# Hybrid decoder layer: weight pairs split inside the softmax, mixer products later, the last head's transposes behind six output products of two token tiles

## Chip, cores and metric

The kernel runs on one core of a Trainium2 chip. The metric is the device time of one execution in microseconds (us). The engines are named as the profile names them: PE (TensorE), PEld (its weight load), DVE (VectorE), ACT (ScalarE), POOL (GpSimd), SP (SyncE, here a queue of DMA issues).

## What is computed

One layer over 512 tokens of 1024 channels, in float32. The part that the change touches is the first sub-layer:

```python
h = rms_norm(x, g_mix_pre)
u, q, k, v = split(h @ w_in)                  # 512 channels each
y_pool = pool_mixer(u, w_pool, pool_scale)    # 4 groups: trailing mean over 2/4/8/16 tokens minus the
                                              # token, then a 128x128 product and a scale per channel
y_attn = moba_attention(q, k, v, rel_bias)    # 8 heads of 64; at 512 tokens: causal attention with bias
x = x + rms_norm(concat(y_pool, y_attn) @ w_out, g_mix_post)
x = x + rms_norm(conv_ffn(rms_norm(x, g_ffn_pre)), g_ffn_post)
x = x + (p @ w_ple) * sigmoid(x @ w_ple_gate)
```

## The kernel before

**Three matmuls for a product.** Every float32 operand is split into a rounded part (hi) and the rest (lo). `mm3` (L222) issues three matmuls for a product: hi and lo crosswise, then hi with hi. For activations `split` (L228) makes the pair: ACT copies the rounded part, DVE subtracts it from the source.

**Weights.** `_Weights` (L68) holds the order of all weight chunks (1 MB each). A chunk is loaded by SP into one of two raw buffers and split in two halves; each half gives a pair (`wh`, `wl`), of which six fit. `ahead(n)` (L122) splits until n pairs lie ahead of the one last taken: a copy on ACT (L147), a subtraction on DVE (L148), and after a chunk's second half the load of the chunk two further on. `take()` hands out the next pair. Pairs 8 to 15 are u0, u1, q2, k2, q3, k3, u2, u3 of the input projection; 16 to 19 are the left half of `w_out` (512 output columns), two blocks of 128 rows in each; 20 to 23 the right half.

**Attention.** There is no scheduler: each engine runs its instructions in the order in which the program issues them. For head h: `scores(h)` (L442) is 8 matmuls on PE, then for the four token tiles on DVE bias, mask and minimum (L454), on ACT the exponential with its sum (L456), on DVE one reciprocal (L457) and four multiplications (L460) that finish the probabilities `L`. `transposes(h)` (L469) turns the ten blocks of `L` on PE into PSUM, and `split` brings them to `PT`. `values(h)` (L486) is 8 matmuls with `V`, and ACT and DVE bring the result into rows of `yT`. Heads come in pairs that share a block of 128 channels: `query` and `key` (L413, L422) project such a pair into `QK`, and `spread` (L429) copies it by DMA to `ST`, from which the scores read.

The loop over h = 0 to 6 (L556) issues the `fills` of h (a projection of 24 matmuls, with which PE passes the time of a softmax; after it `W.ahead(3)`), `transposes(h)`, `scores(h+1)`, and `values(h)`. `pool_in(g)` (L508) projects mixer group g and has POOL make the trailing means; `pool_mid(g)` splits the result, `pool_out(g)` (L529) is the mixer's product (3 matmuls), whose result ACT and DVE bring to block g of `yT`.

**Output product.** `out_part(t, n, ks, ...)` (L571) multiplies token tile t with blocks ks of `w_out` for column half n, three matmuls a block. Blocks 0 to 3 of `yT` are the mixer's, 4 to 7 are heads 0-1, 2-3, 4-5, 6-7. While head 7 is unfinished the blocks `part` = (4, 5, 0, 1, 6) of the four token tiles are multiplied, and after it (2, 3, 7). The order at the end of the attention is:

```python
wo = [W.take() for _ in range(4)]          # L576, after W.ahead(4) behind values(6)
out_part(0, 0, part, True, False)
transposes(H - 1)
out_part(1, 0, part, True, False)
pool_out(2, "pt")
values(H - 1)
pool_mid(3)
out_part(2, 0, part, True, False)
pool_out(3, "pt")
out_part(3, 0, part, True, False)
```

Of the kernel before, what the change touches and what calls it, by code (L numbers as in the profile page):

```python
# [17 lines left out]
F32 = mybir.dt.float32  # L18
F32R = mybir.dt.float32r
# [5 lines left out]
P = 128  # L25
# [42 lines left out]
class _Weights:  # L68
# [31 lines left out]
    def load(self, between=None):  # L100
# [10 lines left out]
        else:  # L111
# [4 lines left out]
            for i in range(n):  # L116
                part = slice(i * step, (i + 1) * step)
                self.nc.sync.dma_start(self.raw[c][:, part, :], src[:, part, :])
                if between is not None:
                    between(i)  # L120

    def ahead(self, n):  # L122

        while self.split < min(self.used + n, 2 * len(self.chunks)):
            c, s = divmod(self.split, 2)
            while self.loaded <= c:
                self.load()
            srcs, axis = self.chunks[c]
            if axis is None:
                view = srcs[s][0]  # L130
            elif axis in (0, 3):
                view = self.raw[c][:, s, :srcs[s].shape[1], :]
            else:
                raw = self.raw[c]
                half = raw.shape[axis] // 2
                part = slice(s * half, (s + 1) * half)
                view = raw[:, part, :] if axis == 1 else raw[:, :, part]
            pair = []
            for kind in "hl":
                t = self.pool.tile([P, 1024], F32R, tag="w" + kind, name=f"w{kind}{self.split}", bufs=self.PAIRS)  # L140
                size = view.shape[1] * view.shape[2]
                pair.append(t[:, :size].rearrange("p (a b) -> p a b", a=view.shape[1]))
            if axis is None:
                for t, src in zip(pair, srcs[s]):
                    self.nc.sync.dma_start(t.bitcast(F32), src)
            else:
                self.nc.scalar.copy(pair[0], view)  # L147
                self.nc.vector.tensor_sub(pair[1], view, pair[0].bitcast(F32))  # L148
            self.pairs[self.split] = pair
            self.split += 1  # L150
            if s == 1:
                self.raw.pop(c, None)
                while self.loaded < min(c + 1 + self.RAW, len(self.chunks)):
                    self.load()

    def take(self):
        self.ahead(1)
# [5 lines left out]
def hybrid_layer(ctx, tc, x, p, rel_bias, g_mix_pre, g_mix_post, g_ffn_pre, g_ffn_post, w_in, w_pool,  # L163
# [23 lines left out]
    for c in (768, 896):  # L187
        W.two(w_in, c, c + 512)
    W.cols(w_in, 256)
    for n in range(2):  # L190
        for k0 in (0, 4):
            W.rows(w_out, k0, 4, 512 * n, 512)
    for fb in range(NF // 2):
        W.cols(w_up, 256 * fb)
        W.cols(w_up, FF + 256 * fb)
# [203 lines left out]
    def project(name, tag="mm", n=3):  # L399
        w = W.take()  # L400
        ps = bank(name, tag)
        for k in range(KD):
            mm3(ps, [q[:, k, :] for q in w], h_moving(k), k == 0, k == KD - 1)
        W.ahead(n)
        return ps
# [4 lines left out]
    QK = ap2.tile([P, 4, S], F32R, name="qk")  # L410
    ST = [[ap2.tile([P, S], F32R, name=f"q_{e}"), ap2.tile([P, 2, S], F32R, name=f"k_{e}")] for e in range(2)]

    def query(hp, spread_now=False):  # L413
        ps = project(f"q{hp}", n=0 if spread_now else 3)
        act.mul(QK[:, 0, :], ps, -(DH ** -0.5))
        dve.scalar_tensor_tensor(QK[:, 3, :], ps, -(DH ** -0.5), QK[:, 0, :].bitcast(F32), op0=ALU.mult,
                                 op1=ALU.subtract)
        if spread_now:
            spread("q")
            W.ahead(3)  # L420

    def key(hp, spread_now=False):  # L422
        ps = project(f"k{hp}", n=0 if spread_now else 3)
        split([QK[:, 1, :], QK[:, 2, :]], ps)
        if spread_now:
            spread("k")
            W.ahead(3)

    def spread(what):  # L429


        for e in range(2):
            src = slice(e * DH, (e + 1) * DH)
            for w in what:
                for a in range(2):
                    dst = ST[e][w == "k"][a * DH:(a + 1) * DH]
                    cs = slice(1, 3) if w == "k" else 0 if a == e else 3
                    sp.dma_start(dst.bitcast(F32), QK[src, cs, :].bitcast(F32))
# [3 lines left out]
    def scores(h):  # L442
        q, k = ST[h % 2]
        bk = [bank(f"s{h}_{b}", "s") for b in range(3)]
        for i, (b, c, _) in place.items():
            n = (i + 1) * P
            for a in (1, 0):
                pe.matmul(bk[b][:, c:c + n], q[:, i * P:n], k[:, a, :n], start=a == 1, stop=a == 0)
        L[h] = ap2.tile([P, 1280], F32, tag="L", name=f"L{h}", bufs=1)
        m = small.tile([P, 12], F32, tag="m", name=f"m{h}", bufs=2)  # L450
        for i, (b, c, o) in place.items():
            n = (i + 1) * P
            l = L[h][:, o:o + n]
            dve.tensor_tensor_reduce(out=l, in0=bk[b][:, c:c + n], in1=T[:, h, S - n:], scale=1.0, scalar=MASKED,  # L454
                                     op0=ALU.add, op1=ALU.min, accum_out=m[:, i:i + 1])
            act.activation(l, l, AF.Exp, bias=m[:, i:i + 1], scale=-1.0, accum_out=m[:, 4 + i:5 + i])  # L456
        dve.reciprocal(m[:, 8:], m[:, 4:8])  # L457
        for i, (b, c, o) in place.items():
            l = L[h][:, o:o + (i + 1) * P]
            dve.tensor_scalar_mul(l, l, m[:, 8 + i:9 + i])  # L460
# [47 lines left out]
    def pool_in(g):  # L508

        w = 2 << g  # L510
        ps = project(f"u{g}", n=4 if g == 2 else 3)
        act.copy(ub[0][:, 16:], ps)  # L512
        src = ub[0]
        for lvl in range(g + 1):
            nxt = ub[1 + lvl % 2]
            pool.tensor_tensor(out=nxt[:, 16:], in0=src[:, 16:], in1=src[:, 16 - (1 << lvl):16 + S - (1 << lvl)],  # L516
                               op=ALU.add)
            src = nxt
        pool.tensor_tensor(out=src[:, 16:16 + w], in0=src[:, 16:16 + w], in1=inv_count[:, :w], op=ALU.mult)
        pool.tensor_scalar(src[:, 16 + w:], src[:, 16 + w:], 1.0 / w, None, op0=ALU.mult)  # L520
        pooled[g] = ap2.tile([P, S], F32, tag="pd", name=f"pd{g}", bufs=2)
        pool.tensor_tensor(out=pooled[g], in0=src[:, 16:], in1=ub[0][:, 16:], op=ALU.subtract)

    def pool_mid(g):
        src = pooled[g]
        pooled[g] = [ap2.tile([P, S], F32R, tag=f"p{i}", name=f"p{i}_{g}", bufs=1) for i in range(2)]
        split(pooled[g], src)

    def pool_out(g, tag="mm"):  # L529
        mp = bank(f"mix{g}", tag)  # L530
        mm3(mp, [q[:, g, :] for q in wp], pooled[g], True, True)
        act.mul(yT[0][:, g, :], mp, pscale[:, g:g + 1])
        dve.scalar_tensor_tensor(yT[1][:, g, :], mp, pscale[:, g:g + 1], yT[0][:, g, :].bitcast(F32),
                                 op0=ALU.mult, op1=ALU.subtract)
# [4 lines left out]
    def y_stationary(t, k):  # L539
        return [q[:, k, t * P:(t + 1) * P] for q in yT]  # L540

    yb = {}
    part = (4, 5, 0, 1, 6)
    query(0, True)
    query(1)
    key(0, True)
    key(1)
    split(wp, wpool)
    scores(0)
    fills = {0: [lambda: pool_in(0)], 1: [lambda: pool_in(1)],  # L550
             2: [lambda: query(2), lambda: pool_out(0)],
             3: [lambda: key(2, True), lambda: query(3), lambda: pool_out(1)],
             4: [lambda: key(3)], 5: [lambda: pool_in(2)],
             6: [lambda: pool_in(3)]}
    after = {1: lambda: pool_mid(0), 2: lambda: pool_mid(1), 6: lambda: pool_mid(2)}
    for h in range(H - 1):  # L556
        for f in fills[h]:
            f()
        transposes(h)
        scores(h + 1)  # L560
        if h in (0, 2, 4):
            spread("q" if h == 2 else "qk")
        values(h)
        if h == H - 2:
            W.ahead(4)
        if h in after:
            after[h]()

# [2 lines left out]
    def out_part(t, n, ks, first, last):  # L571
        if first:
            yb[t, n] = bank(f"y{t}_{n}", "mm" if t < 2 else "s")
        token_product(yb[t, n], t, wo, ks, first, last, y_stationary)

    wo = [W.take() for _ in range(4)]  # L576
    out_part(0, 0, part, True, False)
    transposes(H - 1)
    out_part(1, 0, part, True, False)
    pool_out(2, "pt")  # L580
    values(H - 1)
    pool_mid(3)
    out_part(2, 0, part, True, False)
    pool_out(3, "pt")
    out_part(3, 0, part, True, False)
    at.close()

    res = ctx.enter_context(tc.tile_pool(name="res", bufs=1, reuse_waits="tile"))
# [10 lines left out]
    ya = [op_.tile([P, D], F32, tag="ya", name=f"ya{t}", bufs=4) for t in range(NT)]  # L599
    s0 = []  # L600
    for t in range(NT):
        out_part(t, 0, (2, 3, 7), False, True)
        if t == NT - 1:
            wo = [W.take() for _ in range(4)]
            W.ahead(1)
        junk = op_.tile([P, D], F32, tag="hn", name=f"junk{t}", bufs=2)
        ms = mean_square(yb[t, 0], junk[:, :512], f"msy{t}_0")
        s = op_.tile([P, 1], F32, tag="s0", name=f"s0_{t}", bufs=NT)
        pool.tensor_scalar(s, ms, EPS, None, op0=ALU.add)
        s0.append(s)  # L610
        dve.tensor_mul(ya[t][:, :512], yb[t, 0], g_post[:, :512])
        if t < NT - 1:
            W.ahead(2)
# [459 lines left out]
```

## Time and profile before

| | |
|---|---|
| device time, median of 3 runs | 600.77 us (599.89 to 601.73) |
| device time of the profiled execution | 600.02 us |
| its span, first to last instruction | 598.2 us |
| mean granted TensorE clock | 0.996 |
| PE busy | 584.1 us, 98% of the span |
| DVE, ACT, POOL busy | 71%, 49%, 40% of the span |
| attention, from the first scores to the last transposes | 60.2 to 145.6 us |

In the rows of a timeline the first number is the start in us from the beginning of the span, the second the time to the end of the last instruction of the row (rows that follow each other on an engine are merged, x10 is ten of them). In brackets stands the time that the engine sat idle before the row, and what ended it. Matmuls are pipelined: one of 512 columns is shown with 0.39 us, while they start 0.23 us apart, so that busy time of PE hides gaps of up to 0.16 us.

### The profile page before, as it was taken

To read this page: it belongs to the slowest core of one execution; us is meant where nothing else is said; L and a number is where in the kernel's file an instruction comes from. 1 tells how busy PE (TensorE), PEld (TensorE's weight loads), DVE (VectorE), ACT (ScalarE), POOL (GpSimd) and SP (SyncE) were. 2 spreads that over 40 slices of the span, in tenths; PEclk is the share of its full clock that TensorE was granted. 3 is DMA by queue.
4 is the path that set the end of the run, shared out by engine and by line. 5 is a ranking of instruction groups with operands and counts; after the bars stand their busy time and mean duration, and the time that the engine had idled before them with its cause. 6 is when DMAs were issued, how large, how long until landed. Compare 5 with 4: busy or idle time off the path is not lost.

```text
span 598.2 us, 7479 instructions
## 1 busy us (share of the span) xinstructions
PE 584.1 (98%) x2752; PEld 485.1 (81%) x2752; DVE 425.4 (71%) x556; ACT 293.1 (49%) x476; POOL 236.5 (40%) x236
## 2 busy tenths in 40 slices
PE   8999899997999999999999999999999999999996
PEld 5788788886888998888888888888888878888885
DVE  4724587886378667869755657877878677878985
ACT  6523575664445433433333514534736555766461
POOL 2300330056014559999901696594230000002930
PEclk9999999998999999999999999999999999999999
DMA  8678546533451497999962665776555585752983
GB/s 291 207 269 216 160 116 167 150 108 141 176 165 46 172 374 253 389 328 324 339 211 71 249 202 207 268 270 224 197 182 174 188 280 178 264 196 75 343 267 156
DMA packets 68012, 128.57 MB, mean 215 GB/s; under 512 B 4115, under 2 KB 35439, under 8 KB 66568
## 3 DMA queue, kind: packets, MB, share of 16 engines
q1 hardware_dynamic: 58392, 88.69, 46.0%
q0 software_dynamic: 9584, 39.41, 17.5%
q8 instruction: 21, 0.34, 0.2%
q14 instruction: 15, 0.12, 0.1%
HBM read 97.65 MB, written 26.76 MB: 208 GB/s over the span
## 4 chain that ended last, share of the span: by engine, by line
PE 89%; DVE 4%; ACT 3%; issue 1%; DMA 1%; POOL 0%; SPq 0%; DVEq 0%; ACTq 0%; POOLq 0%
PE gate L225 6%; PE valu L225 6%; PE gate L226 6%; PE valu L226 6%; PE gate L224 6%; PE valu L224 6%; PE d L224 6%; PE d L226 6%; PE d L225 6%; PE y L225 2%; PE y L226 2%; PE y L224 2%; PE g L225 2%; PE g L224 2%; PE g L226 2%; PE o L495 1%
## 5 line engine op out<-in xcount | busy, mean ns | idle before, releaser
L148 DVE TENSOR_TENSOR wl<-raw,wh 128x1024 fp32r<-128x1024 f32 (+1 forms) x118 | 159.0, 1356 | 23.8 <-ACT wh L147 23.3
L147 ACT CAST wh<-raw 128x1024 fp32r<-128x1024 f32 (+1 forms) x118 | 118.4, 1022 | 25.9 <-DMA raw<-in_w_down 9.1
L743 POOL TENSOR_TENSOR b<-b 128x512 f32<-128x512 f32 x60 | 96.0, 1611 | 12.2 <-DMA b<-in_w_down 9.7
L224 PE MATMUL gate<-hT,wl 128*128 128x512 f32 x160 | 62.3, 389 | 0.0
L225 PE MATMUL gate<-hT,wh 128*128 128x512 f32 x160 | 62.3, 389 | 0.0
L226 PE MATMUL gate<-hT,wh 128*128 128x512 f32 x160 | 62.2, 389 | 0.0
L224 PE MATMUL valu<-hT,wl 128*128 128x512 f32 x160 | 62.2, 389 | 0.0
L225 PE MATMUL valu<-hT,wh 128*128 128x512 f32 x160 | 62.2, 389 | 0.0
L226 PE MATMUL valu<-hT,wh 128*128 128x512 f32 x160 | 62.2, 389 | 0.0
L224 PE MATMUL d<-wh,ml 128*128 128x512 f32 x154 | 60.0, 390 | 0.6 <-DVE ml L230 0.6
L226 PE MATMUL d<-wh,mh 128*128 128x512 f32 x154 | 59.9, 389 | 0.0
L225 PE MATMUL d<-wl,mh 128*128 128x512 f32 x154 | 59.9, 389 | 0.0
L254 POOL TENSOR_SCALAR rd<-msd 128x1 f32<-128x1 f32 x4 | 3.4, 861 | 106.4 <-ACT M L249 106.4
L675 ACT ACTIVATE c<-gate,cols 128x512 f32<-128x512 f32 x20 | 15.5, 774 | 59.1 <-PE gate L226 59.1
L516 POOL TENSOR_TENSOR u<-u 128x512 f32<-128x512 f32 x10 | 12.7, 1267 | 75.0 <-ACT u L512 46.0
L687 ACT ACTIVATE sq<-sq 128x512 f32<-128x512 f32 x22 | 13.9, 632 | 48.8 <-DVE sq L686 48.8
L224 PEld LDWEIGHTS valu<-hT,wl 128*128 128x128 f32 x160 | 30.0, 188 | 6.3
L225 PEld LDWEIGHTS valu<-hT,wh 128*128 128x128 f32 x160 | 30.0, 188 | 6.3
L224 PEld LDWEIGHTS gate<-hT,wl 128*128 128x128 f32 x160 | 30.0, 188 | 6.3
L225 PEld LDWEIGHTS gate<-hT,wh 128*128 128x128 f32 x160 | 30.0, 188 | 6.2
L226 PEld LDWEIGHTS gate<-hT,wh 128*128 128x128 f32 x160 | 30.0, 188 | 6.1
L226 PEld LDWEIGHTS valu<-hT,wh 128*128 128x128 f32 x160 | 30.0, 188 | 6.1
(241 smaller groups left out, 1333.8 us busy)
## 6 DMA issues: line engine op xcount, KB each, us to landing
raw<-in_w_up SPq DMA_DIRECT2D x22, 1024.0 KB, 6.6
b<-in_w_down POOLq DMA_DIRECT2D x22, 512.0 KB, 7.3
tsum<-b POOLq DMA_DIRECT2D x11, 1024.0 KB, 6.5
raw<-tsum SPq DMA_DIRECT2D x20, 512.0 KB, 5.4
raw<-in_w_down SPq DMA_DIRECT2D x15, 512.0 KB, 4.8
raw<-in_w_in SPq DMA_DIRECT2D x8, 512.0 KB, 7.5
raw<-in_w_in SPq DMA_DIRECT2D x4, 1024.0 KB, 6.0
k<-qk SPq DMA_DIRECT2D x16, 256.0 KB, 4.5
```

The lines of the kernel that those rows point to most:

```text
L147: self.nc.scalar.copy(pair[0], view)
L148: self.nc.vector.tensor_sub(pair[1], view, pair[0].bitcast(F32))
L224: pe.matmul(o, st[1], mv[0], start=first, stop=False, skip_group_check=more)
L225: pe.matmul(o, st[0], mv[1], start=False, stop=False, skip_group_check=more)
L226: pe.matmul(o, st[0], mv[0], start=False, stop=last, skip_group_check=more)
L254: pool.tensor_scalar(r, ms, add, None, op0=ALU.add)
L495: pe.matmul(o, w, moving(PT[c], j), start=j == 0 and c == 0, stop=j == NT - 1 and c == 1)
L516: pool.tensor_tensor(out=nxt[:, 16:], in0=src[:, 16:], in1=src[:, 16 - (1 << lvl):16 + S - (1 << lvl)], op=ALU.add)
L675: act.activation(c0, pg, AF.Identity, bias=cw[:, 3, f:f + 1], scale=cw[:, 2, f:f + 1])
L687: act.activation(sq, sq, AF.Tanh, scale=GELU_A * GELU_C)
L743: pool.tensor_tensor(out=b[:, o, :], in0=b[:, i0, :], in1=b[:, i1, :], op=ALU.subtract)
```

## The change

A weight pair is no longer split by `W.ahead` after each projection of the attention loop. `ahead` is taken apart into `begin` (buffers and the ACT copy) and `end` (the DVE subtraction, and the load that follows a chunk's second half). `scores` calls `begin` ahead of its four softmax tiles, and `end` between the last of them and the reciprocal: one pair for each head. The projections of the loop split nothing.

At the start the evacuation of the second key projection (`second`) and the split of the mixer's weights go behind `scores(0)`. `pool_out(0)` and `pool_out(1)` go from ahead of the transposes of heads 2 and 3 to between the following head's scores and the values.

At the end `W.ahead(4)` goes. The pairs of `w_out` come in the order of blocks 4-5, 6-7, 0-1, 2-3. Tiles 0 and 1 both get blocks 4, 5, 6 first, tile 0 then 0 and 1; then come `transposes(7)`, blocks 0 and 1 of tile 1, `pool_out(2)`, `values(7)`. Only then the pair of blocks 2-3 is taken (and split). Both remaining tiles' parts go ahead of `pool_out(3)`, and the last blocks run in the order 2, 7, 3.

```diff
+    def begin(self):
+        c, s = divmod(self.split, 2)
+        while self.loaded <= c:
+            self.load()
...
+            self.nc.scalar.copy(pair[0], view)
+        self.pairs[self.split] = pair
+        return axis is not None, pair, view
+
+    def end(self, lo, pair, view):
+        if lo:
+            self.nc.vector.tensor_sub(pair[1], view, pair[0].bitcast(F32))
+        c, s = divmod(self.split, 2)
+        self.split += 1
+        if s == 1:
+            self.raw.pop(c, None)
+            while self.loaded < min(c + 1 + self.RAW, len(self.chunks)):
+                self.load()
...
         while self.split < min(self.used + n, 2 * len(self.chunks)):
+            self.end(*self.begin())
...
-    for n in range(2):
-        for k0 in (0, 4):
-            W.rows(w_out, k0, 4, 512 * n, 512)
+    for k0, n in ((4, 0), (0, 0), (0, 1), (4, 1)):
+        W.rows(w_out, k0, 4, 512 * n, 512)
...
-    def query(hp, spread_now=False):
-        ps = project(f"q{hp}", n=0 if spread_now else 3)
+    def query(hp, spread_now=False, n=0):
+        ps = project(f"q{hp}", n=0 if spread_now else n)
...
+    def key(hp, spread_now=False, n=0):
+        ps = project(f"k{hp}", n=0 if spread_now else n)
+        if not spread_now:
+            return lambda: split([QK[:, 1, :], QK[:, 2, :]], ps)
         split([QK[:, 1, :], QK[:, 2, :]], ps)
...
         m = small.tile([P, 12], F32, tag="m", name=f"m{h}", bufs=2)
+        weights = W.begin()
         for i, (b, c, o) in place.items():
...
             act.activation(l, l, AF.Exp, bias=m[:, i:i + 1], scale=-1.0, accum_out=m[:, 4 + i:5 + i])
+        W.end(*weights)
         dve.reciprocal(m[:, 8:], m[:, 4:8])
...
-        ps = project(f"u{g}", n=4 if g == 2 else 3)
+        ps = project(f"u{g}", n=0)
...
-    part = (4, 5, 0, 1, 6)
-    query(0, True)
-    query(1)
-    key(0, True)
-    key(1)
+    part = (4, 5, 6, 0, 1)
+    query(0, True, 3)
+    query(1, n=3)
+    key(0, True, 3)
+    second = key(1, n=3)
+    scores(0)
+    second()
     split(wp, wpool)
-    scores(0)
     fills = {0: [lambda: pool_in(0)], 1: [lambda: pool_in(1)],
-             2: [lambda: query(2), lambda: pool_out(0)],
-             3: [lambda: key(2, True), lambda: query(3), lambda: pool_out(1)],
-             4: [lambda: key(3)], 5: [lambda: pool_in(2)],
+             2: [lambda: query(2)],
+             3: [lambda: key(2, True), lambda: query(3)],
+             4: [lambda: key(3)()], 5: [lambda: pool_in(2)],
              6: [lambda: pool_in(3)]}
...
             spread("q" if h == 2 else "qk")
+        if h in (2, 3):
+            pool_out(h - 2)
         values(h)
-        if h == H - 2:
-            W.ahead(4)
...
-    wo = [W.take() for _ in range(4)]
-    out_part(0, 0, part, True, False)
+    wo = [None] * 4
+    for i in (2, 3, 0):
+        wo[i] = W.take()
+    for t in range(2):
+        out_part(t, 0, part[:3], True, False)
+    out_part(0, 0, part[3:], False, False)
     transposes(H - 1)
-    out_part(1, 0, part, True, False)
+    out_part(1, 0, part[3:], False, False)
     pool_out(2, "pt")
     values(H - 1)
+    wo[1] = W.take()
     pool_mid(3)
-    out_part(2, 0, part, True, False)
+    for t in range(2, NT):
+        out_part(t, 0, part, True, False)
     pool_out(3, "pt")
-    out_part(3, 0, part, True, False)
...
-        out_part(t, 0, (2, 3, 7), False, True)
+        out_part(t, 0, (2, 7, 3), False, True)
```

## Rows read from the trace of the kernel before

**Rows 1.** The page, part 1: busy time, share, instructions of the engines.

```profile
PE 584.1 (98%) x2752; PEld 485.1 (81%) x2752; DVE 425.4 (71%) x556; ACT 293.1 (49%) x476; POOL 236.5 (40%) x236
```

**Rows 2.** PE's waits, whole span: who waited for whom, us in total, times, longest.

```profile
PE y L225 <- DVE wl L148: 2.1, 1, 2.1
...
PE y L224 <- ACT wh L147: 1.6, 1, 1.6
```

**Rows 3.** One stretch: its length, busy of each engine, granted clock, DMA.

```profile
142.90:146.40 3.50, 3.50 (x14) 3.15 (x15) 1.55 (x3) 1.44 (x3) 1.95 (x4) 0.55 0.77 269
```

**Rows 4.** Timeline of PE around head 0: first and last matmul of u0, transposes(0).

```profile
61.60 0.39 PE L224 MATMUL u<-hT,wl 128*128 128x512 f32 x1
...
66.84 0.39 PE L226 MATMUL u<-hT,wh 128*128 128x512 f32 x1
68.86 1.46 PE L475 MATMUL pt<-ident,L 128*128 128x128 f32 x10 [1.63 <-DVE L L460]
```

**Rows 5.** Timeline of PE: scores(2), scores(4), values(5).

```profile
79.81 1.51 PE L448 MATMUL s<-k,q 128*128 128x512 f32 x8 [0.34 <-issue]
...
105.00 1.52 PE L448 MATMUL s<-k,q 128*128 128x512 f32 x8
...
125.29 1.55 PE L495 MATMUL o<-PT,V 128*128 128x512 f32 x8 [0.18 <-DVE PT L230]
```

**Rows 6.** Timeline of PE from transposes(6) into the output product.

```profile
132.15 1.25 PE L475 MATMUL pt<-ident,L 128*128 128x128 f32 x10
133.16 1.53 PE L448 MATMUL s<-k,q 128*128 128x512 f32 x8
134.52 1.46 PE L495 MATMUL o<-PT,V 128*128 128x512 f32 x8
135.82 0.40 PE L224 MATMUL y<-wh,yT 128*128 128x512 f32 x1
...
147.09 0.39 PE L225 MATMUL y<-wl,yT 128*128 128x512 f32 x1
```

**Rows 7.** Timelines of ACT and DVE: what stands ahead of head 0's softmax.

```profile
62.70 0.59 ACT L229 CAST qk<-k 128x512 fp32r<-128x512 f32 x1 [5.83 <-DMA k<-qk]
...
64.53 0.68 DVE L454 CUSTOM_DVE_ANT_0 L<-s,T 128x512 f32<-128x512 f32 x1
```

**Rows 8.** Timeline of DVE, softmax of head 7: first tile, reciprocal, four multiplications.

```profile
135.07 0.68 DVE L454 CUSTOM_DVE_ANT_0 L<-s,T 128x512 f32<-128x512 f32 x1
...
138.12 0.18 DVE L457 RECIPROCAL m<-m 128x4 f32<-128x4 f32 x1 [1.33 <-ACT L L456]
138.33 1.66 DVE L460 TENSOR_SCALAR L<-L,m 128x512 f32<-128x512 f32 x4
```

**Rows 9.** ACT's groups by shape, 60 to 143 us: busy, mean ns; idle before them.

```profile
L147 ACT CAST wh<-raw 128x1024 fp32r<-128x1024 f32 x9 | 9.2, 1046 | 0.0
...
L456 ACT ACTIVATE L<-L,m 128x512 f32<-128x512 f32 x8 | 5.8, 724 | 13.7 <-DVE m L454 13.7
```

**Rows 10.** Timelines of PE and DVE: last matmul of mixer group 2, its evacuation.

```profile
150.07 0.40 PE L226 MATMUL mix<-p,wp 128*128 128x512 f32 x1
...
151.23 0.75 DVE L533 SCALAR_TENSOR_TENSOR yT<-mix,cols,yT 128x512 fp32r<-128x512 f32 x1 [4.13 <-ACT yT L532]
```

**Rows 11.** DMAs: landing of raw weight chunks; issue and median landing of key 2's spread.

```profile
DMA to landing us min/median/max: 6.2/8.8/12.3
...
99.41 3.17 SPq L438 DMA_DIRECT2D k<-qk  x4
...
k<-qk SPq DMA_DIRECT2D x4, 256.0 KB, 4.5
```

**Rows 12.** Timelines of DVE and POOL: a subtraction beside POOL; POOL's adds for group 3.

```profile
68.98 1.22 DVE L148 TENSOR_TENSOR wl<-raw,wh 128x1024 fp32r<-128x1024 f32 x1
...
69.12 1.98 POOL L516 TENSOR_TENSOR u<-u 128x512 f32<-128x512 f32 x1 [28.56 <-DVE L L460]
...
133.09 4.66 POOL L516 TENSOR_TENSOR u<-u 128x512 f32<-128x512 f32 x4 [2.10 <-ACT u L512]
```

More of the change, by code (lines that the diff above doesn't have):

```diff
@@ L120, in load @@
                     between(i)
+    def begin(self):
+        c, s = divmod(self.split, 2)
+        while self.loaded <= c:
+            self.load()
+        srcs, axis = self.chunks[c]
+        if axis is None:
+            view = srcs[s][0]
+        elif axis in (0, 3):
+            view = self.raw[c][:, s, :srcs[s].shape[1], :]
+        else:
+            raw = self.raw[c]
+            half = raw.shape[axis] // 2
+            part = slice(s * half, (s + 1) * half)
+            view = raw[:, part, :] if axis == 1 else raw[:, :, part]
+        pair = []
+        for kind in "hl":
+            t = self.pool.tile([P, 1024], F32R, tag="w" + kind, name=f"w{kind}{self.split}", bufs=self.PAIRS)
+            size = view.shape[1] * view.shape[2]
+            pair.append(t[:, :size].rearrange("p (a b) -> p a b", a=view.shape[1]))
+        if axis is None:
+            for t, src in zip(pair, srcs[s]):
+                self.nc.sync.dma_start(t.bitcast(F32), src)
+        else:
+            self.nc.scalar.copy(pair[0], view)
+        self.pairs[self.split] = pair
+        return axis is not None, pair, view
@@ L122, in ahead @@
+    def end(self, lo, pair, view):
[7 more added lines that the diff above has]
+                self.load()
     def ahead(self, n):
         while self.split < min(self.used + n, 2 * len(self.chunks)):
-            c, s = divmod(self.split, 2)
-            while self.loaded <= c:
-                self.load()
@@ L128, in ahead @@
[L128 to L154, printed above, removed]
+            self.end(*self.begin())
@@ L419, in query @@
             spread("q")
-            W.ahead(3)
-    def key(hp, spread_now=False):
-        ps = project(f"k{hp}", n=0 if spread_now else 3)
+            W.ahead(n)
+    def key(hp, spread_now=False, n=0):
+        ps = project(f"k{hp}", n=0 if spread_now else n)
+        if not spread_now:
+            return lambda: split([QK[:, 1, :], QK[:, 2, :]], ps)
         split([QK[:, 1, :], QK[:, 2, :]], ps)
@@ L426, in key @@
             spread("k")
-            W.ahead(3)
+            W.ahead(n)
     def spread(what):
```

## The prediction, made before the change was run

> **What bounds the kernel now.** I read the shares of busy time first: PE is busy 98% of the span [rows 1]. The change adds no matmul and removes none, so it can only move what PE waits for and the clock at which it runs. So I read PE's waits next. Two of the longest stand side by side in the first output product, 1.6 us for the rounded half of a weight pair and 2.1 us for its other half [rows 2]; the third is the 1.63 us ahead of the transposes of head 0, for the multiplications that end the softmax [rows 4]. Then I read the clock stretch by stretch. In one of them it is below full: 0.55 between 142.9 and 146.4 us [rows 3], so almost all of it at the lower of the two levels (1.2 instead of 2.4 GHz), directly behind the two weight waits. Last come the timelines of PE, for what a wait really costs, and those of DVE, ACT, POOL and SP, for what would be late in its place.
>
> Two readings are needed throughout. The 24 matmuls of a projection start 0.228 us apart (61.60 to 66.84 in 23 steps) but each is shown as 0.39 us long [rows 4], so a wait of PE is about 0.16 us longer than its idle time. And an undisturbed head takes on PE 1.01 us of transposes, 1.36 of scores and 1.30 of values (the distances of the first four starts of [rows 6]), plus 24 matmuls, 5.5 us: together 9.15 us.
>
> **The last head and the output product.** Before, the four pairs of the left half of `w_out` are split partly behind the softmax of head 7, and the product catches up with them. From the start of the product at 135.82 to 147.09 PE starts 15 matmuls, ten transposes and 4 matmuls more [rows 6]. At full speed that is 19 x 0.23 + 1.01 = 5.4 us; it took 11.27. So this place costs **5.9 us**: 3.6 of idle, some 0.4 that the modelled matmul ends hide, and 1.9 of low clock.
>
> After the change one pair is split per `scores`, beginning with pair 11 in `scores(0)`; `scores(5)`, `(6)` and `(7)` split pairs 16, 17 and 18. The last of these is wanted for block 0 of tile 0, 18 matmuls after `values(6)`. I count from the start of `transposes(6)` as zero: `values(6)` ends at 1.01 + 1.36 + 1.30 = 3.67, block 0 is due at 7.8, and `transposes(7)`, behind 24 matmuls, at 9.2. In the trace of before the softmax of head 7 starts on DVE at 2.92, its reciprocal has waited 1.33 us for the exponentials at 5.97, and its multiplications end at 7.84 [rows 8]. The subtraction, 1.22 us [rows 12], goes into that hole of 1.33 us, so pair 18 is there at about 5.9 and the probabilities at 7.8 to 7.9: 1.9 and 1.3 us early. The ACT copy of 1.05 us lies ahead of the exponentials, where ACT now sits idle 13.7 / 8 = 1.7 us per head [rows 9]. Both waits go, and with them what the clock fell behind. What comes next is `values(7)`: between `transposes(7)` and it lie 6 + 3 matmuls, 2.0 us, against the 1.36 us of scores that lie there in every other head, where the largest wait shown is 0.18 us [rows 5]. I take 0.
>
> The pair of blocks 2-3 is split after `values(7)`, which ends at 9.2 + 1.0 + 1.4 + 0.7 + 1.3 = 13.6. Two evacuations on each engine, the copy and the subtraction make it ready near 17.6; 30 matmuls and `pool_out(3)` run until 21.2. Hidden by 3.6 us. But its subtraction also releases the raw buffer for the last quarter of `w_out`, whose load thus leaves later than now. With the slowest raw landing of the trace, 12.3 us [rows 11], it is in at 29.9 and split at 32.2; PE wants it at 17.6 + 3.6 + 0.4 + 48 x 0.23 = 32.6. Covered, barely at that end, by 3.5 us at the median of 8.8.
>
> **A new wait** stands behind `pool_out(3)`. Before, a whole part of 15 matmuls follows it; after, blocks 2 and 7 of tile 0 do, 6 matmuls, and then block 3, which reads its result as the stationary operand, the DVE half first. For group 2 that half is done at 151.98, 1.91 us after the last mixer matmul started [rows 10]; here block 3 is due 7 x 0.23 = 1.61 after it. That is 0.3 us, and up to one matmul slot more for loading it as stationary: 0.3 to 0.53, I take **0.45**.
>
> **The first softmax.** Before, it stands on ACT and DVE behind the evacuation of the second key projection, which ACT may start only at 62.70, when the spread has read `QK` [rows 7]; so the softmax starts at 64.53, though PE is past the scores at 61.60 [rows 4]. Moved ahead of that, it can start by 61.6 at the latest. In head 7 start to end is 4.92 us [rows 8], which gives 66.5; PE is done with u0 at 66.84 + 0.23 = 67.07. The transposes then start there instead of at 68.86: **1.8 us**. The key's evacuation goes behind the softmax; its readers are the spread for heads 2 and 3, first read at `scores(2)`, more than a head later.
>
> **The middle.** `values(5)` waits 0.18 us for `PT` (0.34 with the hidden part) because two weight subtractions stand ahead of it on DVE; they go away: **0.35**. `scores(2)` has 0.34 us (0.50) that no row explains ("issue") [rows 5]; ends 0 and 0.5, and as the raw load that stood on SP just ahead of that spread now leaves a head earlier, I take **0.5**. Against that, `pool_out(1)` no longer lies between query 3 and `scores(4)`, so the spread of key 2 has 0.7 us less. It is issued from 99.41, two of four issues (0.8 us) are for this head, the median landing is 4.5 [rows 11]: 104.7, where the scores started at 105.0 [rows 5] and would now be due at 104.3. Ends 0 and 0.5, I take **0.2**. On SP the loads now follow the odd pairs, thus `scores(0)`, `(2)`, `(4)` and `(6)`, and the spreads follow `scores(1)`, `(3)` and `(5)`, so no spread is queued directly behind a load that waits for its subtraction; POOL's queue keeps its order. `pool_out(0)` and `(1)` cost PE the same 3 matmuls in either place; their evacuations move behind the multiplications, still 1.3 us ahead of the next transposes. On DVE the rest of a head is lighter by what was in front of `PT`: the multiplications end some 7.3 us after the transposes started, and the next are due at 9.15.
>
> **The sum.** 5.9 + 1.8 + 0.35 + 0.5 - 0.45 - 0.2 = 7.9 us. The profiled execution took 600.02 us (span 598.2), 0.75 below the median of the runs; its span would be 590.3. Against the median of 600.77 that gives **592.9 us**. Everything behind the output product runs relative to PE, which is busy there, and moves with it.
>
> **Rivals.** (a) *POOL holds up the last softmax.* The subtraction of pair 18 now runs beside POOL's seven instructions for mixer group 3. The trace shows that the two disturb each other: an add of POOL issued 0.14 us after such a subtraction took 1.98 us, where the four adds of group 3 took 1.17 each [rows 12]. If the subtraction has to wait for the fourth add, which ends at 133.09 + 4.66 = 137.75, it ends at 138.97, and the softmax 0.85 later, at 8.7: still ahead of 9.2. If each multiplication waits as well, the softmax ends with POOL's work, three more instructions of about 1.17 and thus near 141.3, plus some of its own 1.66 us, at 10 to 10.5: PE waits about 1.2 us, **594.1 us**. For it speaks the 1.98; against it that these multiplications ran beside POOL before too, in 1.66 us. The Trainium skill, "SBUF — State Buffer", section "Who interferes with whom", says that a DVE instruction with two SBUF inputs and a POOL instruction that reads SBUF exclude each other, and the second to issue fully blocks; by it the subtraction does wait for the add, and this rival is what it would make of the rest. The 1.98 us agrees with it.
>
> (b) *The first softmax stays late*, because its bias rows, its scores or its weight copy are not there in time: without the 1.8 us it is **594.7 us**. Nothing in the rows shows such a lateness; DVE simply ran these in order.
>
> (c) *The late wait moves.* If PE waits as long at `transposes(7)`, or for pair 18, as it did for the weights, and the clock falls again, the 5.9 stay: 600.77 - 2.0 = **598.8 us**. It takes 3 us more than the spare 1.3; no row has that.
>
> (d) *Slower: ACT waits for raw weights ahead of the exponentials.* `begin` puts a copy in front of every softmax; if its chunk has not landed, the exponentials, the reciprocal behind the subtraction, and the transposes wait. A head has 9.15 - 7.3 = 1.85 us to spare. To lose the 7.9 and 2.1 more (**602.9 us**) each of seven heads must be late by 1.85 + 10 / 7 = 3.3 us. The load of a chunk leaves three heads, 27 us, ahead of its copy, and the slowest landing is 12.3 [rows 11]; it decides from about 30 us on.
>
> **How the numbers follow.** The forecast has 0.70, (a) 0.12, (b) 0.08, (c) 0.05, (d) 0.05. About 0.3% (1.8 us) is what a measurement of this kernel can tell from no change. Faster by more than that are the forecast, (a), (b) and half of (c), less a remainder of 0.02: 0.91. Within it: half of (c) and 0.02, 0.05. Slower: 0.04 of (d). The range: if nothing new waits, the gain is 8.55, 592.2, and runs of before spread 0.9 below and above; low 591.2. Upwards it takes in (a) and (b) with that spread, 596.0.
>
> **What would show it.** Right: no wait of `y` for `wl` or `wh`; the clock at full in every stretch of the attention; `transposes(0)` one matmul slot behind u0; the subtraction between L454 and the reciprocal, and the reciprocal's idle time gone; a wait of a few tenths of `y` for DVE (L533). Wrong: a wait of `pt` for L460 at head 6 or 7 (a), ACT waiting for raw (d), or a clock below 1 behind any of them (c).

## The result, and the profile after

The changed kernel takes **592.03 us** (median of 4 runs, 591.28 to 592.42) against 600.85 us (4 runs, 599.89 to 601.73). The ratio is 0.9852, with a 95% interval of 0.9834 to 0.9870: 8.8 us faster. The forecast was 592.9 with a range from 591.2 to 596.0. The kernel before takes near 600.2 us in most executions and near 601.8 in the others, so that a ratio, which goes by all of them, and a difference of medians part by some tenths.

In the changed file the lines have moved: L233 to L235 are the three matmuls, L146 and L153 the two halves of a weight split, L459 the scores, L466, L468, L470 and L473 the softmax, L488 the transposes, L508 the values, L546 the mixer's evacuation.

The page of the kernel after, part 1 (busy time) and the head of part 4 (the chain of work that ended last, as shares of the span by engine), is to be read beside [rows 1]:

```profile
span 590.7 us, 7481 instructions
...
PE 582.8 (99%) x2752; PEld 485.3 (82%) x2752; DVE 426.3 (72%) x556; ACT 292.3 (49%) x476; POOL 235.7 (40%) x236
...
PE 97%; DVE 1%; DMA 1%; ACT 1%; issue 0%; POOL 0%; SPq 0%; DVEq 0%; POOLq 0%
```

The same line of part 4 in the kernel before:

```profile
PE 89%; DVE 4%; ACT 3%; issue 1%; DMA 1%; POOL 0%; SPq 0%; DVEq 0%; ACTq 0%; POOLq 0%
```

The number of matmuls is the same, and all busy times are to within 1.3 us. What changed is the chain: it now runs through PE for 97% of the span instead of 89%. PE's waits of the kernel after, whole span (us in total, times, longest), beside [rows 2]:

```profile
PE idle L327 <- POOL ident masks.py:199: 1.4, 1, 1.4
PE d L233 <- DVE ml L239: 0.6, 1, 0.6
PE s L459 <- DMA k<-qk: 0.5, 1, 0.5
PE y L233 <- DVE yT L546: 0.2, 1, 0.2
```

No wait for `wl` or `wh` is left, none for the softmax, and the one new wait is the one that was forecast behind the last mixer product. The clock is 1.00 in every stretch from 60 to 166 us; here is the one of the same time as [rows 3], which holds later instructions now (the columns are the stretch, its length, PE, PEld, DVE, ACT, POOL busy, granted clock, DMA share, GB/s):

```profile
142.90:146.40 3.50, 3.50 (x19) 2.96 (x18) 2.02 (x3) 2.82 (x5) 1.60 (x3) 1.00 0.87 320
```

The timeline of PE after: `transposes(0)`, `transposes(6)` and the first product, `transposes(7)`, and the place of the new wait:

```profile
61.43 1.55 PE L459 MATMUL s<-k,q 128*128 128x512 f32 x8 [0.45 <-DMA k<-qk]
62.82 0.40 PE L233 MATMUL u<-hT,wl 128*128 128x512 f32 x1
...
68.27 1.25 PE L488 MATMUL pt<-ident,L 128*128 128x128 f32 x10
...
129.91 1.25 PE L488 MATMUL pt<-ident,L 128*128 128x128 f32 x10
...
133.58 0.40 PE L233 MATMUL y<-wh,yT 128*128 128x512 f32 x1
...
139.09 1.25 PE L488 MATMUL pt<-ident,L 128*128 128x128 f32 x10
...
152.38 0.40 PE L235 MATMUL y<-wh,yT 128*128 128x512 f32 x1
152.96 0.50 PE L233 MATMUL y<-wh,yT 128*128 128x512 f32 x1 [0.18 <-DVE yT L546]
153.29 0.40 PE L234 MATMUL y<-wl,yT 128*128 128x512 f32 x1
```

A stretch of PE's program that holds the same instructions in both kernels runs from the scores of head 0 to the transposes of `pin` behind the output product (at 172.98 us before and 165.44 after). Split at the transposes of heads 0 and 6 it gives where the time went:

| from ... to | before | after | gained | forecast |
|---|---|---|---|---|
| first matmul of u0 to `transposes(0)` | 7.26 | 5.45 | 1.81 | 1.8 |
| `transposes(0)` to `transposes(6)` | 63.29 | 61.64 | 1.65 | 0.65 (0.35 + 0.5 - 0.2) |
| `transposes(6)` to the transposes of `pin` | 40.83 | 35.53 | 5.30 | 5.45 (5.9 - 0.45) |
| sum | | | 8.76 | 7.9 |

The spans differ by 7.5 us only, because in this execution of the changed kernel the first 61 us, which the change does not touch, took 1.2 us longer; the medians agree with the sum of the table.

### The profile page after: what moved, and what is told of

It reads as the page before. It is cut to its first block, busy times and chain, and to the rows that moved or that the text cites. A ratio compares the mean times of both kernels' runs of the same rounds, so it can differ in the third digit from the quotient of the medians.

```text
span 590.7 us, 7481 instructions
## 1 busy us (share of the span) xinstructions
PE 582.8 (99%) x2752; PEld 485.3 (82%) x2752; DVE 426.3 (72%) x556; ACT 292.3 (49%) x476; POOL 235.7 (40%) x236
## 4 chain that ended last, share of the span: by engine, by line
PE 97%; DVE 1%; DMA 1%; ACT 1%; issue 0%; POOL 0%; SPq 0%; DVEq 0%; POOLq 0%
PE gate L233 6%; PE valu L233 6%; PE valu L235 6%; PE gate L234 6%; PE gate L235 6%; PE valu L234 6%; PE d L233 6%; PE d L235 6%; PE d L234 6%; PE y L233 2%; PE y L235 2%; PE y L234 2%; PE g L234 2%; PE g L233 2%; PE g L235 2%; PE s L459 2%
## 5 line engine op out<-in xcount | busy, mean ns | idle before, releaser
L153 DVE TENSOR_TENSOR wl<-raw,wh 128x1024 fp32r<-128x1024 f32 (+1 forms) x118 | 159.4, 1358 | 21.6 <-ACT wh L146 21.1
L146 ACT CAST wh<-raw 128x1024 fp32r<-128x1024 f32 (+1 forms) x118 | 118.8, 1024 | 24.1 <-DMA raw<-in_w_down 7.9
L233 PE MATMUL gate<-hT,wl 128*128 128x512 f32 x160 | 62.3, 389 | 0.0
L235 PE MATMUL gate<-hT,wh 128*128 128x512 f32 x160 | 62.2, 389 | 0.0
L233 PE MATMUL valu<-hT,wl 128*128 128x512 f32 x160 | 62.2, 389 | 0.0
L235 PE MATMUL valu<-hT,wh 128*128 128x512 f32 x160 | 62.2, 389 | 0.0
L233 PE MATMUL d<-wh,ml 128*128 128x512 f32 x154 | 60.0, 390 | 0.6 <-DVE ml L239 0.6
L235 PE MATMUL d<-wh,mh 128*128 128x512 f32 x154 | 59.9, 389 | 0.0
L529 POOL TENSOR_TENSOR u<-u 128x512 f32<-128x512 f32 x10 | 10.6, 1064 | 73.7 <-ACT u L525 73.2
L695 DVE SCALAR_TENSOR_TENSOR c<-gate,cols,c 128x511 f32<-128x511 f32 x20 | 14.9, 746 | 29.2 <-ACT c L694 29.2
L235 PEld LDWEIGHTS gate<-hT,wh 128*128 128x128 f32 x160 | 30.0, 188 | 6.3
L235 PEld LDWEIGHTS valu<-hT,wh 128*128 128x128 f32 x160 | 30.0, 188 | 6.3
L233 PEld LDWEIGHTS valu<-hT,wl 128*128 128x128 f32 x160 | 30.0, 188 | 6.2
L233 PEld LDWEIGHTS gate<-hT,wl 128*128 128x128 f32 x160 | 30.0, 188 | 6.2
```

The lines of the kernel that those rows point to most:

```text
L233: pe.matmul(o, st[1], mv[0], start=first, stop=False, skip_group_check=more)
L235: pe.matmul(o, st[0], mv[0], start=False, stop=last, skip_group_check=more)
L695: dve.scalar_tensor_tensor(c0[:, 1:], pg[:, :S - 1], cw[:, 1, f:f + 1], c0[:, 1:], op0=ALU.mult, op1=ALU.add)
```

## Experiments

The kernel before is the reference of every run; its median was 600.43 us beside the first four, 600.46 beside the two with the subtraction ahead of the softmax and without POOL's work, and 600.56 beside the others. The changed kernel was run again beside these others.

**The start alone** (the kernel before, plus):

```diff
-    key(1)
-    split(wp, wpool)
-    scores(0)
+    second = key(1, later=True)
+    scores(0)
+    second()
+    split(wp, wpool)
```

> The kernel before, with the start alone changed: scores and softmax of head 0 issued ahead of the second key's evacuation and of the split of the mixer's weights. My step: the 1.79 us ahead of the first transposes go, and 0.2 us of slower transposes behind them: 1.8 to 2.0 us less, 598.9 us. Rival (b), that the first softmax is late for another reason (its scores, its bias rows): no change, 600.9 us, and the wait of pt for the multiplications stays.

Measured: 599.0 us, ratio 0.9975 (0.9963 to 0.9986), 1.4 us less by the medians and 1.5 by the ratio. No wait of `pt` is left, and u0 to `transposes(0)` is 5.5 us. So rival (b) falls. Part of the gain was given back at the end of the attention, where the waits for weights are unchanged but the low clock lasted longer: this trace shows all of 5 us at half, where [rows 3] have 0.55 over 3.5 us, and from `transposes(6)` to `pin` it takes 41.80 us instead of 40.83.

```profile
140.94:145.98 5.04, 5.04 (x17) 4.37 (x18) 2.25 (x4) 1.54 (x3) 1.98 (x4) 0.50 0.93 310
```

**The end alone** (the kernel before, with the new order of the `w_out` pairs and of the products; splits still behind the projections):

```diff
-    for n in range(2):
-        for k0 in (0, 4):
-            W.rows(w_out, k0, 4, 512 * n, 512)
+    for k0, n in ((4, 0), (0, 0), (0, 1), (4, 1)):
+        W.rows(w_out, k0, 4, 512 * n, 512)
...
-        if h == H - 2:
-            W.ahead(4)
...
+    for i in (2, 3, 0):
+        wo[i] = W.take()
...
```

> The kernel before, with the end alone changed: order of the w_out pairs, order of the output products, last pair taken behind the values of head 7; weight pairs are split behind each projection as before. Theory A: the late waits came from the order, since with the splits of before pairs 16 to 18 are ready by head 6 and only the fourth, with block 6 in it, was late; then nearly the whole 5.9 goes less the new wait of 0.45: 595.4 us, clock at full. Theory B, as the prediction put it: the pairs come in time because one is split within each softmax; then a wait of y for wl or wh stays here and the time is 598 us or more.

Measured: 596.01 us, ratio 0.9921 (0.9905 to 0.9936), 4.4 us less by the medians and 4.7 by the ratio. PE's longest waits in this kernel, in which the matmuls' and softmax' lines stand one lower than before:

```profile
PE pt L474 <- DVE L L459: 1.6, 1, 1.6
...
PE y L223 <- DVE yT L532: 0.2, 1, 0.2
```

The wait ahead of `transposes(0)` is still there, the weight waits are gone, and from `transposes(6)` to `pin` it takes 169.49 - 134.06 = 35.43 us, as in the changed kernel. So theory A holds: **the order alone removes the late waits**. With the splits of before three of the four pairs are ready by head 6, as the subtractions in the kernel before show: those of the first three end by 124.63, ahead of `transposes(6)` at 132.15.

```profile
113.13 1.23 DVE L148 TENSOR_TENSOR wl<-raw,wh 128x1024 fp32r<-128x1024 f32 x1
...
122.29 2.34 DVE L148 TENSOR_TENSOR wl<-raw,wh 128x1024 fp32r<-128x1024 f32 x2
...
141.60 1.21 DVE L148 TENSOR_TENSOR wl<-raw,wh 128x1024 fp32r<-128x1024 f32 x1
```

Late was only the fourth, and the old order had put block 6, which is wanted ahead of `transposes(7)`, into it; the new order puts blocks 2 and 3 there, which are wanted last. The edit has two parts that were not run one by one, the order of the pairs and the 24 instead of 15 matmuls ahead of `transposes(7)`; the second is priced below, at 1.4 us in the changed kernel.

**The split in the softmax alone** (the kernel before, with `begin` and `end` in `scores`, and no splits behind the loop's projections; all orders as before):

```diff
+        weights = W.begin()
         for i, (b, c, o) in place.items():
...
+        W.end(*weights)
         dve.reciprocal(m[:, 8:], m[:, 4:8])
```

> The kernel before, with the splits alone changed: one weight pair within each head's softmax, none behind the projections; start, mixer products and end in the order of before. Theory A: only the small waits in the middle go (0.35 of values 5, 0.5 of scores 2, some tenths of slow starts), 0.9 to 1.4 us, 599.6 us, and the late weight waits stay, because the fourth pair, with block 6, is still split behind the values of head 6. Theory B: the late waits go too, 594 to 595 us.

Measured: 600.66 us, ratio 1.0016 (0.9999 to 1.0032): nothing, where 0.9 to 1.4 us were expected. Its waits show why:

```profile
PE y L235 <- DVE wl L153: 2.9, 2, 2.7
PE pt L489 <- DVE L L474: 2.6, 2, 2.4
...
PE mix L235 <- DVE p L240: 0.7, 1, 0.7
```

The places of the two long ones in PE's timeline:

```profile
70.83 0.40 PE L489 MATMUL pt<-ident,L 128*128 128x128 f32 x1 [2.41 <-DVE L L474]
71.45 2.18 PE L489 MATMUL pt<-ident,L 128*128 128x128 f32 x9 [0.21 <-DVE L L474]
...
142.11 0.50 PE L235 MATMUL y<-wl,yT 128*128 128x512 f32 x1 [2.65 <-DVE wl L153]
```

A late wait stayed, as theory A had it, but at another pair than the theory named. The 2.65 us stand at the second matmul of block 4, the first of the product: its pair, the third, is now subtracted in the softmax of head 7 (139.98 to 142.06). The fourth pair costs only 0.24 us. And where PE waits for a softmax, as for that of head 0 here, the subtraction inside it is not free: the wait went from 1.6 to 2.4 us. Behind this wait the granted clock was 0.56 from 70.8 to 72.0 us and 0.50 from 72.0 to 74.0, and from `transposes(0)` to `(1)` it took 11.06 us instead of 9.36. A mixer product of the old place now waits for its operand, too. These took back what was gained from `transposes(2)` to `(6)` (42.73 us instead of 43.54) and behind them (40.02 instead of 40.83). The profiled execution took 602.37 us, 1.7 more than the median, so its sums are not those of every execution.

**Work in place of the two waits** (the kernel before, plus 16 matmuls whose result nobody uses):

```diff
-    out_part(0, 0, part, True, False)
+    out_part(0, 0, part[:4], True, False)
+    idle = bank("hold", "s")
+    for _ in range(16):
+        pe.matmul(idle, yT[0][:, 4, :P], yT[0][:, 4, :], start=True, stop=True)
+    out_part(0, 0, part[4:], False, False)
     transposes(H - 1)
```

> The kernel before, with 16 added matmuls of 512 columns (16 x 0.23 = 3.7 us, their result is not used) ahead of block 6 of token tile 0, so that PE works where it waited for the weights. If the low clock from 142.9 to 146.4 us comes from those two waits and costs 1.9 us, as the sum has it, the time falls by 1.9 to 598.9 us although PE does more, and the clock stays at full. If the low clock has another cause (the transposes, the DMA burst that starts there), the time stays at 600.9 us and the stretch still shows about 0.55.

Measured: 599.29 us, ratio 0.9975 (0.9964 to 0.9986): with more work on PE the kernel is 1.1 to 1.5 us faster. The clock is full, and the transposes of head 7 take 1.0 us again:

```profile
139.51 3.81 PE L580 MATMUL hold<-yT 128*128 128x512 f32 x16
143.16 0.40 PE L224 MATMUL y<-wh,yT 128*128 128x512 f32 x1
143.80 0.50 PE L225 MATMUL y<-wl,yT 128*128 128x512 f32 x1 [0.24 <-DVE wl L148]
144.14 0.40 PE L226 MATMUL y<-wh,yT 128*128 128x512 f32 x1
144.38 1.25 PE L475 MATMUL pt<-ident,L 128*128 128x128 f32 x10
...
142.90:146.40 3.50, 3.26 (x20) 2.48 (x20) 2.16 (x4) 1.33 (x3) 2.72 (x6) 1.00 0.65 201
```

From `transposes(6)` to `pin` it takes 172.28 - 133.09 = 39.19 us against 40.83. The low clock came from the two waits, and it cost 1.6 us in these traces, where the sum had 1.9.

**The changed kernel as it is**, beside three of those below:

> The changed kernel as it is, beside the three that follow, so that they can be compared on one chip: 592.0 us.

Measured: 591.94 us. The profiled execution took 595.74 us, since PE waited 3.3 us in the second key projection, which the change does not touch. Behind it the three rows of the table come out as before: 5.48, 61.63 and 35.56 us.

**The changed kernel without the split in the softmax** (both of the first two edits together):

> The changed kernel without the split in the softmax: start and end of the changed kernel, but weight pairs split behind each projection and mixer products where they were before. Theory A: the split in the softmax is worth only the small delays in the middle, 1.4 us between the transposes of heads 0 and 6 in the two traces, so 593.4 us. Theory B: the splits in the softmax carry the gain at the end, 596 us or more. Theory C: they are worth nothing, 592.0 us.

Measured: 593.54 us in the middle of three executions (592.57 to 593.59), 1.6 us above the changed kernel. That is theory A: the split in the softmax is worth the small delays in the middle and no more. The edit also puts the two mixer products back to their old places, so the 1.6 us are of both, and no trace shows in which heads they lie.

**The transposes of head 7 behind 15 matmuls** (the changed kernel, with):

```diff
-    for t in range(2):
-        out_part(t, 0, part[:3], True, False)
-    out_part(0, 0, part[3:], False, False)
+    out_part(0, 0, part, True, False)
     transposes(H - 1)
-    out_part(1, 0, part[3:], False, False)
+    out_part(1, 0, part, True, False)
```

> The changed kernel with transposes of head 7 behind the five blocks of token tile 0 alone (15 matmuls), as before, instead of behind 24. By my step the transposes are due at 1.01 + 1.36 + 1.30 + 15 x 0.23 = 7.1 us after those of head 6, and the softmax of head 7 ends 8.7 after them in the changed trace: PE waits 1.5 us, 593.5 us; the clock stays up if that wait is not longer than the 1.8 us of head 0 in the kernel before, which it survived. Rival: the cover is not needed, 592.0 us.

Measured: 593.34 us, 1.4 above the changed kernel. The size was right; the place is two places, as the timeline of PE shows:

```profile
136.24 0.51 PE L234 MATMUL y<-wl,yT 128*128 128x512 f32 x1 [0.59 <-DVE wl L153]
...
138.22 1.28 PE L488 MATMUL pt<-ident,L 128*128 128x128 f32 x10 [0.53 <-DVE L L473]
```

PE first waits for the pair of blocks 0-1, whose subtraction stands in DVE's softmax of head 7, and then for that softmax. The nine matmuls of the other tile are cover for both.

**The subtraction ahead of the softmax** (the changed kernel, with):

```diff
-        weights = W.begin()
+        W.end(*W.begin())
...
-        W.end(*weights)
```

> The changed kernel with each head's weight subtraction ahead of the four softmax tiles on DVE instead of between them and the reciprocal. If the hole in which DVE waits for the exponentials is what makes the split free, every softmax now ends 1.2 us later, and more beside POOL: in a plain head at 8.4 to 8.7 us after its transposes, still ahead of the next at 9.14, so no wait there; in head 7 at 9.7 to 10, where the transposes are due at 9.2: PE waits 0.5 to 0.9 us, 592.7 us. Rival: a head has so much to spare that the place in DVE's order does not matter, 592.0 us.

Measured: 594.04 us, ratio 0.9885 (0.9868 to 0.9903): 2.1 us above the changed kernel (on another chip; 2.2 by the distances to the kernel before), where 0.7 was expected. Its waits:

```profile
PE pt L487 <- DVE L L472: 0.9, 1, 0.9
PE s L459 <- DMA k<-qk: 0.8, 2, 0.5
...
PE q L233 <- DVE yT L545: 0.2, 1, 0.2
```

The wait at head 7 is as expected: `transposes(7)` come 10.37 us after `transposes(6)` instead of 9.18. Not expected were two more, at heads 2 and 3, together 1.3 us (15.94 instead of 15.26 from the transposes of head 2 to those of head 3, 10.41 instead of 9.82 to those of head 4): with the softmax later, the evacuation of the mixer product behind it is later, for which query 3 waits to get its PSUM bank, and the spread of key 2, for which the scores of head 4 wait. A plain head can hide 1.2 us more on DVE; those two can't.

**No POOL work beside the last softmax** (the changed kernel; left out are the trailing means of mixer group 3, whose pooled rows are zeros):

```diff
+        if g == 3:
+            pooled[g] = ap2.tile([P, S], F32, tag="pd", name=f"pd{g}", bufs=2)
+            pool.memset(pooled[g], 0.0)
+            return
         for lvl in range(g + 1):
```

> The changed kernel with POOL's trailing means of mixer group 3 left out (its input is set to zero), so that POOL is quiet during the softmax of head 7. If the weight subtraction there took 2.11 us instead of 1.22 because POOL reads SBUF beside it, it takes 1.22 now, and the four multiplications about 1.28 instead of 1.89: the softmax of head 7 ends 1.0 to 1.5 us earlier. The time does not change (592 us), since the softmax had 0.5 us to spare. Rival: the subtraction is slow for another reason (its weight copy, the DMA) and stays near 2.1.

Measured once: 591.91 us. DVE's softmax of head 7 in the changed kernel, with the split in the middle, and POOL beside it:

```profile
134.47 2.11 DVE L153 TENSOR_TENSOR wl<-raw,wh 128x1024 fp32r<-128x1024 f32 x1
136.50 0.17 DVE L470 RECIPROCAL m<-m 128x4 f32<-128x4 f32 x1
136.70 1.89 DVE L473 TENSOR_SCALAR L<-L,m 128x512 f32<-128x512 f32 x4
...
130.85 4.65 POOL L529 TENSOR_TENSOR u<-u 128x512 f32<-128x512 f32 x4 [2.84 <-ACT u L525]
135.57 1.08 POOL L532 TENSOR_TENSOR u<-u,inv_count 128x16 f32<-128x16 f32 x1
136.72 1.66 POOL L533 TENSOR_SCALAR u<-u 128x496 f32<-128x496 f32 x1
```

and the same lines of DVE without POOL's work:

```profile
134.03 1.22 DVE L153 TENSOR_TENSOR wl<-raw,wh 128x1024 fp32r<-128x1024 f32 x1
135.44 0.18 DVE L470 RECIPROCAL m<-m 128x4 f32<-128x4 f32 x1 [0.19 <-ACT L L468]
135.65 1.28 DVE L473 TENSOR_SCALAR L<-L,m 128x512 f32<-128x512 f32 x4
```

The subtraction falls from 2.11 to 1.22 us and the multiplications from 1.89 to 1.28. The softmax ends 7.46 us after `transposes(6)` began instead of 8.68, and the time does not move, since PE asks for it at 9.18.

**The last mixer product earlier** (the changed kernel, with):

```diff
-    for t in range(2, NT):
-        out_part(t, 0, part, True, False)
-    pool_out(3, "pt")
+    out_part(2, 0, part, True, False)
+    out_part(3, 0, part[:3], True, False)
+    pool_out(3, "pt")
+    out_part(3, 0, part[3:], False, False)
```

> The changed kernel with the last mixer product between blocks 4, 5, 6 and blocks 0, 1 of token tile 3, so that 12 matmuls (2.7 us) instead of 6 lie between it and block 3. My step: the new wait of 0.45 us goes, 591.6 us, and PE has no wait left in the output product. Rival: its operand comes from POOL and is not split in time at the earlier place, so the wait only moves, 592.0 us or more.

Measured: 591.18 us in the middle of five executions (590.75 to 591.55) against 591.94 of the changed kernel on the same chip (591.22 to 595.74). The ranges overlap, but the trace settles it: no wait of `y` is left anywhere in the span, and `transposes(7)` to `pin` takes 164.22 - 138.35 = 25.87 us instead of 26.35, which is 0.48 less. It is the fastest of all the kernels here.

## Why the prediction was right, point by point

- **The last head and the output product**: forecast 5.9, measured 5.30 + 0.45 = 5.75. Right in size and in its two parts, the waits and the clock (1.6 us by the added matmuls, 1.9 in the sum). **Wrong in its cause**: the prediction let the pairs come in time because one is split within each softmax. The end alone does it, with the splits left where they were, and the split alone makes the third pair late. The step that failed is the sentence that "the product catches up" with the splits: it caught up with one pair, the fourth, which held block 6, wanted ahead of `transposes(7)`. That is to be read off the list of chunks and the order of the blocks; I had read only which engine PE waited for. The size came out all the same because it was taken from the trace of before, where it does not depend on what removes the waits.
- **The first softmax**: forecast 1.8, measured 1.81, with nothing late in its place. Another 0.21 us that came with it stands in the next row of the table: behind their wait the ten transposes took 1.22 us to the start of the scores (68.86 to 70.08), and now take 1.01. DVE starts it at 62.20, 0.77 after the scores, and is through 1.5 us ahead of PE.
- **The middle**: forecast 0.65, measured 1.65, the term that was mis-sized. Of the 1.0 us of difference, 0.2 was set aside for the spread of key 2, which did not come at all: `scores(4)` start 1.01 us after their transposes. The two waits that were counted gave 0.14 more than their 0.85. The rest, 0.66 us, lies where no wait is shown: 0.22 from `transposes(0)` to `(1)`, 0.20 from those of head 2 to those of head 4 (the moved mixer products taken out), 0.24 from head 4 to 5. The first is the quicker transposes of head 0: the start alone has it too, with 63.08 us instead of 63.29 from `transposes(0)` to `(6)`. So the middle gave 1.43, and what the sum put at nothing is the other 0.44: delays too short to appear as idle time behind matmuls that are drawn 0.16 us too long. The spread of key 2 is close all the same: the experiment with the subtraction in front turned it into a wait.
- **The new wait** behind the last mixer product: forecast 0.45 for DVE's half of its result, measured 0.35 ahead of the first matmul of block 3 (152.38 to 152.96, less 0.23) and 0.10 behind it.
- **The hole of 1.33 us**: right. Outside POOL's activity DVE idles 0.19 us ahead of the reciprocal instead of 1.33, and the experiment that took the subtraction out of the hole lost 2.1 us.
- **Rival (a), POOL beside the last softmax**: half of it happened. The subtraction did take 2.11 us, and ends at 136.58, 1.08 us behind the end of POOL's fourth add (130.85 + 4.65 = 135.50). The softmax ended 8.68 us after the start of `transposes(6)`; the prediction gave 8.7 for just this case and 9.2 for when it is needed, so PE does not notice. The Trainium skill, "SBUF — State Buffer", section "Who interferes with whom", has the second of two such instructions fully blocked; the trace and the run without POOL agree for this subtraction beside POOL's add. They do not for every one: the subtraction of head 6 was issued in the same trace 0.09 us behind POOL's scaling and ended 0.20 us behind it, where a full block would have made it 2.6 us long (126.63 - 125.25 + 1.22, an estimate).

```profile
125.25 1.58 DVE L153 TENSOR_TENSOR wl<-raw,wh 128x1024 fp32r<-128x1024 f32 x1
...
125.16 1.47 POOL L533 TENSOR_SCALAR u<-u 128x504 f32<-128x504 f32 x1
```

The multiplications of head 7, which read one tensor and a column, took 1.89 us while POOL's scaling ran 1.66 us beside them: 0.61 more than without POOL, and not held until it ended.
- **Rivals (b), (c), (d)** did not happen: no wait for the first softmax, no late wait and no low clock in the attention, no ACT wait for raw weights that reached PE. That a late chunk would decide from some 30 us on was argued from the landing times and was not tried.

By the ratios the start alone is worth 1.5 us, the end alone 4.7, the split alone nothing; together they give 8.9. The missing 2.7 is in the main the middle (1.6, which the split and the moved mixer products give only once nothing waits for head 0's softmax) and the low clock, which cost the start alone 1.0 us more in its trace.

## What to carry to other kernels

When PE waits for a prepared operand, look first at which one it is and whether the order of use could ask for it last; here that gave more than half of the gain without moving any work between engines. Filling a hole in a dependent chain with independent work is free only where the chain's end has time to spare: the same subtraction, with the moved mixer products, was worth 1.6 us in the finished kernel, nothing as a single edit, and it took 2.11 us instead of 1.22 beside POOL. A wait on PE is to be priced with the clock behind it, and matmuls that start closer than they are drawn hide the first 0.16 us of every wait, so distances between the same instructions in two traces tell more than idle times.

## What the runs showed of the hardware that I had not expected

The clock's loss is not a fixed charge: behind the same two waits (1.55 and 2.07 us with one matmul between them) it was 0.55 over 3.5 us in the kernel before and 0.50 over at least 5 us in the one with the start alone, and it did not fall at all behind the single wait of 1.63 us ahead of `transposes(0)` [rows 4], where it was 1.00 from 68.9 to 72.0 us. Behind the wait of 2.41 us that the split alone had in the same place it fell to 0.50, so it does not take two waits. Added matmuls without any use made the kernel 1.1 us faster. And the disturbance between DVE and POOL goes both ways: POOL's 16-column multiplication took 1.08 us beside the subtraction of head 7, where it took 0.22 in the kernel before with no subtraction beside it.
